# A two-layer encoder on one core: half of the low parts of the up weights subtracted on GpSimd instead of VectorE

## The chip, the cores and the metric

The kernel runs on one core of a Trainium2 chip. A core has TensorE (PE) for matrix products with its own weight loads (PEld), VectorE (DVE), ScalarE (ACT), GpSimd (POOL) and SyncE (SP), which mostly issues DMAs. The metric is the device time of one execution in microseconds (us), of which the median over the runs is taken. Lower is better.

## The reference

The computation is an encoder trunk on 256 tokens of width 2048, with two layers, all in float32:

```python
m = rms_norm(mem, mem_norm)
for i in range(2):
    n = rms_norm(h, attn_norm[i])
    # layer 0: neighbourhood attention, layer 1: grouped-query attention, both beside
    # cross attention from the tokens to 256 memory tokens
    ...
    h = h + concatenate([mix, cross]) @ w_o[i]
    n = rms_norm(h, mlp_norm[i])
    h = h + square(relu(n @ w_up[i])) @ w_down[i]     # 2048 -> 8192 -> 2048
return rms_norm(h, final_norm)
```

The change lies in the MLP, in `n @ w_up[i]`, which runs once in each layer.

## The kernel before

**Precision by splitting.** Products are made in the type fp32r. Each float32 operand is split in two: `hi`, a copy in fp32r made by ScalarE, and `lo`, the difference between the source and `hi`, made by VectorE. A product is then the sum of three: hi*hi, hi*lo and lo*hi. The helper `split` (lines 477 to 480) issues both instructions: line 479 on ScalarE, line 480 on VectorE. So line 480 stands for the low parts of all operands, and the tile names tell them apart.

**The MLP.** The weights of `w_up` come as 64 chunks a layer, each 128x2048 floats in the tile `raw_U` (1 MB, one DMA from SP's queue, line 951). A chunk is used in two halves of 128x1024. `half_of_side` (line 943) takes a pair of tiles `uh` and `ul` for a half, with two buffers for each name, and splits the half of `raw_U` into them. The products of a chunk are 48 matrix products at line 384: for each of 16 blocks, `hi` with two parts of the activations `hT` and `lo` with one, summed in `ps_u`. Behind it ScalarE applies relu and square (lines 1019 and 1020, tile `c`).

Six chunks run ahead (`LEAD = 6`). From then on the kernel works in steps, 58 in each layer. A step has four grains in this order: the first products of a pair chunk of `w_down`, the first and the second half of an up chunk, and the second products of the pair chunk. The pair chunks are computed by Strassen's scheme: four weight blocks `b` (1 MB by DMA) are combined into seven, three of them sums `t` made by VectorE (lines 1072, 1074 and 1075) and one by an accumulating DMA that GpSimd issues (line 1073, `b<-b`). The four blocks in `b` are split into `bh` and `bl`, the three sums into `th` and `tl` (one buffer each). The first grain has 12 products with `bh` and `bl`, the last has 9 with `th` and `tl`. On every second step VectorE also makes four combinations `c` (line 1030) and the split of `a_s`. Steps go in runs (`RUNS`, eight in each layer); at the end of a run the seven PSUM sums are taken over by VectorE (lines 1144 and 1155) and ScalarE (line 1157).

**What sets the order.** Each grain has stages `load`, `pre` and `prep`, which are traced some grains before it runs (`ahead`); the splits of an up half are traced four grains ahead. The order on each engine is then chosen by the scheduler, which simulates the engines' times; `past` and `issue_after` tie some instructions behind others on the same engine. Each engine works its queue in order, and waits in it for what an instruction needs.

Of the kernel before, what the change touches and what calls it, by code (L numbers as in the profile page):

```python
# [10 lines left out]
F32 = mybir.dt.float32  # L11
# [3 lines left out]
ALU = mybir.AluOpType  # L15
# [19 lines left out]
HALF = CH // 2  # L35
# [122 lines left out]
def encoder_kernel(ctx: ExitStack, tc: tile.TileContext, t: dict, out: bass.AP):  # L158
    nc = tc.nc
# [3 lines left out]
    def opened(name, side="left", space=None, bufs=1):  # L163
        kw = {"space": space} if space else {}
        manager = tc.tile_pool(name=name, bufs=bufs, side=side, reuse_waits="tile", **kw)
        pools[name] = manager, manager.__enter__()
        return pools[name][1]

    def closed(*names):
        for name in names:  # L170
            pools.pop(name)[0].__exit__(None, None, None)
# [31 lines left out]
    first = const.tile([P, GAINS + NT * D], F32, name="first")  # L203
# [43 lines left out]
    def halves_of(w):  # L247
# [6 lines left out]
        def prep_early(hf):  # L254
            if w.early == "ring":

                tiles[hf] = new_half(w.kind)
                box["early", hf] = split(*tiles[hf], tiles["raw"][:, hf * HALF : (hf + 1) * HALF])
            else:
                tiles[hf] = half_of_side(tiles["raw"], hf, MOVING_AT)  # L260
# [111 lines left out]
    def products(ps, acts, k0, nk, hi, lo, keep_order=False, first=None):  # L372

        for j in range(nk):
            k = k0 + j
            s = slice(j * P, (j + 1) * P)
            parts = [(hi, slice(0, SEQ)), (hi, slice(SEQ, 512)), (lo, slice(0, SEQ))]
            if k == KT - 1:
                parts[:2] = parts[1::-1]
            elif j == 0 and isinstance(lo, Entered):  # L380
                parts = parts[2:] + parts[:2]
            for n, (x, part) in enumerate(parts):
                x = first if n == j == 0 and first is not None else x[:, s]
                ins = nc.tensor.matmul(ps, x, acts[:, k, part], start=k == n == 0,  # L384
                                       stop=k == KT - 1 and n == 2)
                if keep_order and n == 0:
                    pin(ins)
# [86 lines left out]
            plan.append(Work("M", blocks[b][0][c], acts, c * 4, begins, last, start, blocks[b][1]))  # L474


    def split(dst_hi, dst_lo, src):

        first = nc.scalar.activation(dst_hi, src, AF.Copy)  # L479
        return first, nc.vector.tensor_tensor(dst_lo, src, dst_hi.bitcast(F32), op=ALU.subtract)  # L480

    def rstd_of(ss, n, name):

# [456 lines left out]
    FIRST = ("p3", 6, 0), ("p1", 0, 1), ("p2", 2, 2), ("p5", 3, 3)  # L940
    SECOND = ("p7", 4, 0), ("p6", 5, 1), ("p4", 1, 2)

    def half_of_side(raw, hf, place=0):
        s = slice(place // 4, place // 4 + HALF)
        tiles = tuple(at.side.tile([P, HALF + 64], F32R, tag=n, bufs=2, name=n)[:, s] for n in ("uh", "ul"))
        box.setdefault("splits", []).append(split(*tiles, raw[:, hf * HALF : (hf + 1) * HALF]))
        return tiles

    def loaded(src, tag):
        raw = at.side.tile([P, CH], F32, tag=tag, bufs=2, name=f"raw_{tag}")  # L950
        nc.sync.dma_start(raw, src)
        return raw

    def up_grains(layer, m):
        own = {}
        lead = m < LEAD

        def load():
            own["raw"] = loaded(t[f"w_up{layer}"][m], "U")

        def prep(hf):

            with tc.issue_after(box["summed"].ins) if m in (1, 2) else nullcontext():
                prepared(hf)

        def prepared(hf):
            half = 2 * m + hf
            if lead and (half in (2, 4) or half > 4 and half % 3 == 2):

                if half < 5:  # L970
                    room = at.side.tile([P, 2, HALF], F32R, tag="b", bufs=2, name="u_b")
                    own[hf] = room[:, 0], room[:, 1]
                else:
                    s = slice(U_AT // 4, U_AT // 4 + HALF)
                    own[hf] = tuple(at.mlp.tile([P, 3 * 512], F32R, tag=x, name=f"u_{x}")[:, s] for x in ("th", "tl"))
                box["splits"].append(split(*own[hf], own["raw"][:, hf * HALF : (hf + 1) * HALF]))
            else:
                own[hf] = half_of_side(own["raw"], hf)
            if not lead and hf == 0:

                room = at.side.tile([P, 256], F32R, tag="junk", bufs=1, name="u_0")
                own["first"] = room[:, COPY_AT // 4 :][:, :P]
                nc.scalar.activation(own["first"], own["raw"][:, :P], AF.Copy)

        def run(hf):
            if m == hf == 0:
                closed("cat", "ring")
                at.mlp = opened("mlp")
                box["z"] = [at.mlp.tile([P, 4, 512], F32, tag=f"z{q}", name=f"z{q}") for q in range(2)]
                box["z_set"] = set()  # L990

                last = at.mlp.tile([P, 14 * P], F32R, tag="a", bufs=6, name="hT_l")[:, LAST_COPY_AT // 4 :][:, :SEQ]
                nc.scalar.activation(last, box["hT"][:, KT - 1, :SEQ].bitcast(F32), AF.Copy)
                box["hT0"] = Plain(box["hT"], last)
            if hf == 0:
                if lead:
                    own["ps"] = at.acc.tile([P, 512], F32, tag="acc", name="ps_u")[:, :SEQ]
                else:
                    own["ps"] = sum_of("up")[:, :SEQ]

            with tc.issue_after(box["late"].ins) if m == hf == 0 else nullcontext():
                products(own["ps"], box["hT0" if lead else "hT"], hf * (KT // 2), KT // 2, *own.pop(hf),
                         keep_order=not lead, first=own.pop("first", None))

        def after():
            squared(layer, m, own["ps"])

        soon = (8, 8, 3) if m == 1 else SOONER
        return [Grain(lambda: run(0), None, load, None, lambda: prep(0), soon),
                Grain(lambda: run(1), after, None, None, lambda: prep(1), SOONER)]  # L1010

    def squared(layer, m, ps):

        e = m % 2
        if e == 0:
            box["c"] = at.mlp.tile([P, 8, P], F32, tag="c", bufs=2, name="c")
        c = box["c"]
        two = c[:, 2 * e : 2 * e + 2, :].rearrange("p a b -> p (a b)")
        nc.scalar.activation(two, ps, AF.Relu)
        nc.scalar.activation(two, two, AF.Square)  # L1020
        if e == 0:
            return
        pair = m // 2
        if pair >= max(STEPPED):
            a = at.mlp.tile([P, 2, 4, P], F32R, tag="a", bufs=6, name="a_p")
            split(a[:, 0], a[:, 1], c[:, :4])
        else:
            for d, x, y, op in ((4, 2, 0, ALU.subtract), (5, 1, 0, ALU.add), (6, 5, 2, ALU.subtract),
                                (7, 3, 6, ALU.subtract)):
                box["made"] = nc.vector.tensor_tensor(c[:, d, :], c[:, x, :], c[:, y, :], op=op)  # L1030
            a = at.mlp.tile([P, 2, 7, P], F32R, tag="a", bufs=6, name="a_s")
            split(a[:, 0], a[:, 1], c[:, 1:])
            if pair >= min(STEPPED):

                n = pair - min(STEPPED)
                if n == 0:
                    box["a_0"] = at.mlp.tile([P, max(STEPPED) - min(STEPPED), 2, P], F32R, tag="a", bufs=6, name="a_0")
                split(box["a_0"][:, n, 0], box["a_0"][:, n, 1], c[:, 0])
        box["a", pair] = a
        if m == UPS - 1 and layer == 1:  # L1040
            later(2, load_gf)
# [91 lines left out]
    def sum_of(name):  # L1133
        if name in box["unused"]:
            box["unused"].remove(name)
        else:
            box["ps"][name] = at.sums.tile([P, 512], F32, tag=name, name="ps_u" if name == "up" else name)
        return box["ps"][name]
# [39 lines left out]
    def plain_grains(layer, nb, at_chunk):  # L1178
# [9 lines left out]
        def prep(c, hf):  # L1188
            if (at_chunk + c) % 2 == 0:
                own[c, hf] = half_of_side(own[c], hf, MOVING_AT)  # L1190
            else:
                own[c, hf] = tuple(at.mlp.tile([P, HALF], F32R, tag="bt"[hf] + x, name=f"{x}_p") for x in "hl")
                box["rest"] = split(*own[c, hf], own[c][:, hf * HALF : (hf + 1) * HALF])
# [450 lines left out]
```

## Time and profile before

| | |
|---|---|
| runs | 2001.65 and 2002.13 us, median 2001.89 |
| span of the profiled execution | 1999.8 us, 2.1 us less than the median; the profile gives no other time of this execution |
| TensorE busy in the span | 1989.3 us (99%), 12920 products |
| VectorE busy | 1724.4 us (86%) |
| ScalarE busy | 1276.3 us (64%) |
| GpSimd busy | 123.4 us (6%), of which 100.6 us are 116 DMA issues |
| `ul` subtractions on VectorE | 262, mean 1217 ns, 318.1 us |

Times are those of one profiled execution. A row of a timeline gives the start and the duration of an instruction in us, its engine, the line of the kernel, and the tile it writes `<-` the tiles it reads; behind it, in brackets, how long the engine stood idle before it and what ended the wait. A row of groups gives the number of instructions, their busy time and mean duration, and the idle time before them.

### The profile page before, as it was taken

To read this page: it belongs to the slowest core of one execution; us is meant where nothing else is said; L and a number is where in the kernel's file an instruction comes from. 1 tells how busy PE (TensorE), PEld (TensorE's weight loads), DVE (VectorE), ACT (ScalarE), POOL (GpSimd) and SP (SyncE) were. 2 spreads that over 40 slices of the span, in tenths; PEclk is the share of its full clock that TensorE was granted. 3 is DMA by queue.
4 is the path that set the end of the run, shared out by engine and by line. 5 is a ranking of instruction groups with operands and counts; after the bars stand their busy time and mean duration, and the time that the engine had idled before them with its cause. 6 is when DMAs were issued, how large, how long until landed. Compare 5 with 4: busy or idle time off the path is not lost.

```text
span 1999.8 us, 32844 instructions
## 1 busy us (share of the span) xinstructions
PE 1989.3 (99%) x12920; PEld 1806.9 (90%) x12920; DVE 1724.4 (86%) x2140; ACT 1276.3 (64%) x1735; POOL 123.4 (6%) x145
## 2 busy tenths in 40 slices
PE   9999999999999999999999999999999999999998
PEld 8999999899999999999998888889999999999987
DVE  6777777579998999999999778778998999999997
ACT  6655555467666666666666556666676666666664
POOL 0000000000000000000000001000000000000000
PEclk9999999999999999999999999999999999999999
DMA  7856665757777777777676765557777777777773
GB/s 290 313 192 204 209 208 189 258 175 244 231 228 232 236 234 237 218 238 234 211 232 226 232 234 169 194 177 255 229 227 235 218 235 235 232 239 227 225 227 133
DMA packets 105707, 448.02 MB, mean 224 GB/s; under 512 B 10960, under 2 KB 38608, under 8 KB 58064
## 3 DMA queue, kind: packets, MB, share of 16 engines
q1 hardware_dynamic: 88560, 414.99, 59.4%
q0 software_dynamic: 16704, 30.42, 9.0%
q8 instruction: 101, 1.65, 0.3%
q10 hardware_dynamic: 288, 0.52, 0.1%
q14 instruction: 54, 0.44, 0.1%
HBM read 398.17 MB, written 4.19 MB: 201 GB/s over the span
## 4 chain that ended last, share of the span: by engine, by line
PE 97%; DMA 1%; DVE 1%; issue 1%; ACT 0%; SPq 0%; DVEq 0%; POOLq 0%; POOL 0%; ACTq 0%
PE ps_u L384 34%; PE p L1103 9%; PE p L1104 9%; PE p L1101 9%; PE ps_s L384 9%; PE ps_m L361 8%; PE ps_m L364 8%; PE ps_m L365 8%; DMA raw_l<-in_w_km 0%; PE sc_ps L537 0%; PE sc_ps L538 0%; PE sc_ps L536 0%; PE av L611 0%; PE av L612 0%; PE av L610 0%
## 5 line engine op out<-in xcount | busy, mean ns | idle before, releaser
L384 PE MATMUL ps_u<-hT,uh 128*128 128x256 f32 x3812 | 663.0, 276 | 0.0
L384 PEld LDWEIGHTS ps_u<-hT,uh 128*128 128x128 f32 x3812 | 578.6, 188 | 5.5
L384 PE MATMUL ps_u<-hT,ul 128*128 128x256 f32 x1960 | 541.3, 276 | 0.0
L479 ACT ACTIVATE uh<-raw_U 128x1024 fp32r<-128x1024 f32 x262 | 277.9, 1061 | 238.0 <-PE ps_u L384 226.2
L384 PEld LDWEIGHTS ps_u<-hT,ul 128*128 128x128 f32 x1960 | 368.0, 188 | 0.0
L480 DVE TENSOR_TENSOR lo<-raw,hi 128x1024 fp32r<-128x1024 f32 (+1 forms) x215 | 254.0, 1189 | 96.7 <-ACT hi L479 96.0
L480 DVE TENSOR_TENSOR ul<-raw_U,uh 128x1024 fp32r<-128x1024 f32 x262 | 318.1, 1217 | 19.0 <-ACT uh L479 18.9
L479 ACT ACTIVATE hi<-raw 128x1024 fp32r<-128x1024 f32 (+1 forms) x215 | 221.5, 1036 | 160.6 <-PE ps_m L365 80.8
L479 ACT ACTIVATE bh<-b 128x2048 fp32r<-128x2048 f32 x116 | 222.9, 1922 | 101.5 <-PE p L1104 90.5
L480 DVE TENSOR_TENSOR bl<-b,bh 128x2048 fp32r<-128x2048 f32 x116 | 265.2, 2286 | 12.7 <-ACT bh L479 12.7
L480 DVE TENSOR_TENSOR tl<-t,th 128x1536 fp32r<-128x1536 f32 x116 | 203.4, 1754 | 39.3 <-ACT th L479 38.4
L479 ACT ACTIVATE th<-t 128x1536 fp32r<-128x1536 f32 x116 | 172.9, 1490 | 43.6 <-PE p L1104 41.0
L1103 PE MATMUL p<-bl,a_s 128*128 128x512 f32 x464 | 180.9, 390 | 0.5 <-DVE bl L480 0.3
L1104 PE MATMUL p<-bh,a_s 128*128 128x512 f32 x464 | 181.3, 391 | 0.0
L1101 PE MATMUL p<-bh,a_s 128*128 128x512 f32 x464 | 180.6, 389 | 0.0
L1073 POOL DMA_DIRECT2D b<-b x116 | 100.6, 867 | 1146.9 <-DVE t L1072 939.0
L384 PE MATMUL ps_s<-nT,hi 128*128 128x256 f32 x896 | 154.7, 276 | 0.0
L1101 PE MATMUL p<-th,a_s 128*128 128x512 f32 x348 | 136.1, 391 | 0.0
L1103 PE MATMUL p<-tl,a_s 128*128 128x512 f32 x348 | 135.8, 390 | 0.0
L384 PEld LDWEIGHTS ps_s<-nT,hi 128*128 128x128 f32 x896 | 135.5, 188 | 0.2
L1104 PE MATMUL p<-th,a_s 128*128 128x512 f32 x348 | 135.4, 389 | 0.0
L384 PE MATMUL ps_s<-nT,lo 128*128 128x256 f32 x448 | 123.7, 276 | 0.0
(294 smaller groups left out, 3524.2 us busy)
## 6 DMA issues: line engine op xcount, KB each, us to landing
raw_U<-in_w_up SPq DMA_DIRECT2D x128, 1024.0 KB, 4.9
b<-in_w_pair SPq DMA_DIRECT2D x116, 1024.0 KB, 4.9
raw<-in_w_o SPq DMA_DIRECT2D x32, 1024.0 KB, 5.0
b<-b POOLq DMA_DIRECT2D x116, 256.0 KB, 3.4
raw<-in_w_b SPq DMA_DIRECT2D x21, 1024.0 KB, 5.0
raw<-in_w_av SPq DMA_DIRECT2D x12, 1024.0 KB, 4.9
raw<-in_w_aq SPq DMA_DIRECT2D x12, 1024.0 KB, 5.0
raw<-in_w_ak SPq DMA_DIRECT2D x12, 1024.0 KB, 4.8
```

Of the source, the lines that this page charges most:

```text
L361: first = nc.tensor.matmul(ps, ah, hi[:, s], start=st, stop=False)
L364: nc.tensor.matmul(ps, ah, lo[:, s], start=False, stop=False)
L365: final = nc.tensor.matmul(ps, al, hi[:, s], start=False, stop=sp)
L384: ins = nc.tensor.matmul(ps, x, acts[:, k, part], start=k == n == 0, stop=k == KT - 1 and n == 2)
L479: first = nc.scalar.activation(dst_hi, src, AF.Copy)
L480: return first, nc.vector.tensor_tensor(dst_lo, src, dst_hi.bitcast(F32), op=ALU.subtract)
L1073: nc.gpsimd.dma_start(b[:, 3, :], b[:, 1, :], accum_op=ALU.add)
L1101: ins = nc.tensor.matmul(ps, a[:, 0, ai, :], hi[:, s], start=begins, stop=False)
L1103: nc.tensor.matmul(ps, a[:, 0, ai, :], lo[:, s], start=False, stop=False)
L1104: nc.tensor.matmul(ps, a[:, 1, ai, :], hi[:, s], start=False, stop=ends)
```

## The change

`split` and `half_of_side` take an engine for the subtraction, and `up_grains` passes GpSimd for the second half (`hf` is 1) of the chunks that are not among the first six. 58 chunks in each of two layers are concerned. The copy to `uh` stays on ScalarE, and the buffers, the products and the first half stay as they are.

```diff
-    def split(dst_hi, dst_lo, src):
+    def split(dst_hi, dst_lo, src, engine=None):
 
         first = nc.scalar.activation(dst_hi, src, AF.Copy)
-        return first, nc.vector.tensor_tensor(dst_lo, src, dst_hi.bitcast(F32), op=ALU.subtract)
+        engine = engine or nc.vector
+        return first, engine.tensor_tensor(dst_lo, src, dst_hi.bitcast(F32), op=ALU.subtract)
...
-    def half_of_side(raw, hf, place=0):
+    def half_of_side(raw, hf, place=0, engine=None):
         s = slice(place // 4, place // 4 + HALF)
         tiles = tuple(at.side.tile([P, HALF + 64], F32R, tag=n, bufs=2, name=n)[:, s] for n in ("uh", "ul"))
-        box.setdefault("splits", []).append(split(*tiles, raw[:, hf * HALF : (hf + 1) * HALF]))
+        box.setdefault("splits", []).append(split(*tiles, raw[:, hf * HALF : (hf + 1) * HALF], engine))
         return tiles
...
             else:
-                own[hf] = half_of_side(own["raw"], hf)
+                own[hf] = half_of_side(own["raw"], hf, engine=nc.gpsimd if hf and not lead else None)
```

## The prediction

> **What bounds the kernel now.** I begin with the page's busy times and the chain that ended last, to see whose time the end is.
>
> ```profile
> PE 1989.3 (99%) x12920; PEld 1806.9 (90%) x12920; DVE 1724.4 (86%) x2140; ACT 1276.3 (64%) x1735; POOL 123.4 (6%) x145
> ...
> PE 97%; DMA 1%; DVE 1%; issue 1%; ACT 0%; SPq 0%; DVEq 0%; POOLq 0%; POOL 0%; ACTq 0%
> ```
>
> TensorE is the bound: 1989.3 of 1999.8 us, and 97% of the chain. VectorE carries 1% of it, so taking work off VectorE can win at most a little: 1999.8 - 1989.3 = 10.5 us of idle PE is all there is, 0.5%. The open question is what the change costs. For that the stage counts where the changed line runs, so the second view is the table by stretches: two long stretches of the MLP (one per layer), and one pair of steps.
>
> ```profile
> core 0: us, PE busy (x) PEld busy (x) DVE busy (x) ACT busy (x) POOL busy (x), PEclk, DMA share, GB/s
> 500.00:1000.00 500.00, 500.00 (x3377) 459.04 (x3375) 465.43 (x502) 336.43 (x374) 42.60 (x49) 1.00 0.73 230
> 1400.00:1900.00 500.00, 500.00 (x3374) 459.01 (x3373) 465.39 (x504) 336.41 (x374) 42.15 (x49) 1.00 0.74 230
> 541.25:561.71 20.46, 20.46 (x140) 18.79 (x139) 18.29 (x20) 13.69 (x16) 1.74 (x2) 1.00 0.72 229
> ```
>
> PE never rests here and its clock is full. VectorE is busy 465.4 of 500 us, so it is the second bound: a step of one up chunk and one pair chunk takes 20.46 / 2 = 10.23 us, in which VectorE works 10.23 x 465.4 / 500 = 9.52 us and rests 0.71 us. From the order of VectorE's work in that pair of steps:
>
> ```profile
> 547.34 1.21 DVE L480 TENSOR_TENSOR ul<-raw_U,uh 128x1024 fp32r<-128x1024 f32 x1
> 548.48 0.68 DVE L1075 TENSOR_TENSOR t<-t,b 128x512 f32<-128x512 f32 x1
> 549.08 1.22 DVE L480 TENSOR_TENSOR ul<-raw_U,uh 128x1024 fp32r<-128x1024 f32 x1
> 550.21 0.28 DVE L1030 TENSOR_TENSOR c<-c 128x128 f32<-128x128 f32 x1
> 551.48 1.76 DVE L480 TENSOR_TENSOR tl<-t,th 128x1536 fp32r<-128x1536 f32 x1 [0.99 <-ACT th L479]
> ...
> 554.65 2.29 DVE L480 TENSOR_TENSOR bl<-b,bh 128x2048 fp32r<-128x2048 f32 x1
> ...
> 559.12 1.23 DVE L480 TENSOR_TENSOR ul<-raw_U,uh 128x1024 fp32r<-128x1024 f32 x1 [0.44 <-ACT uh L479]
> 560.26 0.81 DVE L1030 TENSOR_TENSOR c<-c 128x128 f32<-128x128 f32 x3
> ```
>
> The second `ul` of each step (549.08 and 559.12) is the one that the change moves. Each frees 550.21 - 549.08 = 1.13 us of VectorE's line (an instruction starts 0.08 us before the one ahead of it ends). Almost everything else in the line is a tensor_tensor with both inputs in SBUF.
>
> **The change part by part.** *Removed from VectorE:* 58 chunks behind the first six in each of two layers, 116 subtractions by 1.13 us, 131 us in all, or 1.13 us a step. None of it lies on PE's chain, so alone it is worth nothing.
>
> *Added on GpSimd:* 116 subtractions of 128x1024. No row shows such an instruction there. What GpSimd does show:
>
> ```profile
> L227 POOL MEMSET ones<- 128x128 f32 x1 | 0.2, 204 | 0.3 <-POOLq L1634 0.3
> L229 POOL MEMSET mhalf<- 128x8 f32 x1 | 0.1, 104 | 0.0
> ```
> ```profile
> L1407 POOL TENSOR_SCALAR b_r_r<-b_r_r,rstd x8: 302/436/1369, 1135.5 to 1228.3; 128x4 f32<-128x4 f32 x8
> ```
>
> From the two memsets one stream costs (204 - 104) / 120 = 0.83 ns an element, 0.85 us for 1024, and the shortest small two-operand instruction gives 0.30 us to start and end. If the two inputs and the output all run beside one another, that is 1.15 us; if the inputs follow each other, 2.0 us; if all three do, 2.85 us. Ends 1.15 and 2.85; the rows do not say whether the store hides, and I take the middle of the upper two, 2.4 us. [...]
>
> *Does it run beside VectorE?* If it did, GpSimd's 6% load would take it in easily. These rows speak against it:
>
> ```profile
> 405.40 0.69 POOL L852 TENSOR_TENSOR scale<-near,mhalf 128x2 f32<-128x2 f32 x1 [333.09 <-DVE near L836]
> ...
> 1094.66 3.88 POOL L1298 TENSOR_TENSOR rstd<-full,mhalf 128x2 f32<-128x2 f32 x1 [65.57 <-DVE full L836]
> ```
> ```profile
> 1094.47 1.23 DVE L480 TENSOR_TENSOR lo<-raw,hi 128x1024 fp32r<-128x1024 f32 x1
> 1095.61 1.23 DVE L480 TENSOR_TENSOR ul<-raw_U,uh 128x1024 fp32r<-128x1024 f32 x1
> 1096.74 1.23 DVE L480 TENSOR_TENSOR lo<-raw,hi 128x1024 fp32r<-128x1024 f32 x1
> 1098.58 0.17 DVE L1454 TENSOR_SCALAR qm_s<-rstd 128x2 f32<-128x2 f32 x1 [0.60 <-POOL rstd L1298]
> ```
>
> The same power of two numbers takes 0.69 us with VectorE idle and 3.88 us when three subtractions run on VectorE without a gap. It ends at 1098.54, 0.57 us after the last of them (1097.97). So GpSimd waits for a gap in VectorE's two-input work, and most of its 0.69 us still lies ahead of it then; some 0.12 us of its start is hidden by the wait. Whether VectorE in turn waits while GpSimd reads is what the sum hangs on. One row leans against it:
>
> ```profile
> 1227.12 1.04 POOL L488 TENSOR_TENSOR b_r_r<-b_r_v,mhalf 128x4 f32<-128x4 f32 x1 [0.92 <-DVE b_r_v L486]
> ```
> ```profile
> 1227.83 0.69 DVE L1412 TENSOR_TENSOR b_o<-b_y,cos_q 128x512 f32<-128x512 f32 x1 [0.79 <-ACT b_y L1410]
> ```
>
> Here a VectorE product starts inside a GpSimd instruction and is not stretched; but that one reads four numbers a partition, which it may have done long before 1227.83. The bounds for VectorE's wait are 0 and the whole hold. I take the whole hold, as an engine that is kept off something by its neighbour most likely keeps the neighbour off as well.
>
> [...]
>
> *The sum.* Per step VectorE loses 2.4 - 0.12 = 2.28 us to the hold and 0.08 us of overlap at the break, and is spared 1.13: a net 1.23 us. It has 0.71 us of rest, so 0.52 us a step do not fit: 116 x 0.52 = 60 us. Against that stands the lead with which VectorE now works. `bl` ends at 554.65 + 2.29 = 556.94; the product that reads it:
>
> ```profile
> L1103 PE MATMUL p<-bl,a_s 128*128 128x512 f32 x464 | 180.9, 390 | 0.5 <-DVE bl L480 0.3
> ```
> ```profile
> 549.99 0.39 PE L1103 MATMUL p<-bl,a_s 128*128 128x512 f32 x1
> ```
>
> The first read of the next `bl` comes a period later, at 560.2, 3.3 us after its making; two layers give 2 x 3.3 = 7 us of lag for free. VectorE's work from PSUM at the ends of runs may partly go on during a hold:
>
> ```profile
> L1144 DVE SCALAR_TENSOR_TENSOR first<-p,inv,first 128x512 f32<-128x512 f32 x48 | 35.8, 746 | 3.1 <-PE p L1104 1.1
> L1155 DVE TENSOR_TENSOR z<-p,z 128x512 f32<-128x512 f32 x48 | 32.8, 684 | 1.1 <-PE p L1104 1.1
> ```
>
> That is 68.6 us in 16 bursts of 4.3 us; each burst could hide 1 us of a hold, but also spends more than the 3.3 us lead at once, and I set the two against each other. The sum: 60 - 7 = +53 us. The profiled span is 1999.8 us, so 2053; the median of the runs is 2.1 us longer than this span, so the time shown should be **2055 us**, +2.6%.
>
> *Queues and covers.* The subtraction waits on GpSimd for `uh` (ACT), and behind it stands the accumulating DMA of the next pair chunk (L1073), for which ACT's `bh` waits.
>
> ```profile
> 554.50 0.87 POOL L1073 DMA_DIRECT2D b<-b  x1 [8.48 <-DVE t L1072]
> ```
> ```profile
> b<-b POOLq DMA_DIRECT2D x116, 256.0 KB, 3.4
> ```
> ```profile
> 558.02 1.06 ACT L479 ACTIVATE uh<-raw_U 128x1024 fp32r<-128x1024 f32 x1 [1.66 <-PE ps_u L384]
> ...
> 562.91 1.92 ACT L479 ACTIVATE bh<-b 128x2048 fp32r<-128x2048 f32 x1 [0.40 <-PE p L1104]
> ```
>
> GpSimd rested 8.48 us ahead of that issue; a subtraction from 559.1 to 561.5 is over before the next issue near 565, and the landed data (554.50 + 3.4 = 557.9) waits 5 us for `bh`. I cost the queue at nothing; with the subtraction more than 5 us late the DMA, `bh`, `bl` and PE are late in turn. The subtraction's own latency is covered too:
>
> ```profile
> 552.65 5.45 PE ps_u L384 x48
> ```
>
> The up products of a chunk take 5.45 us, so the second half starts at 552.65 + 2.72 = 555.4, and a step later at 565.6, 4 us behind the subtraction's end at 561.5. SP's queue and ACT's work are unchanged.
>
> **The rivals.** *(A) Forecast:* both exclude each other and the sum overflows VectorE's rest. With the subtraction between 2.1 and 2.65 us the time is 2020 to 2085; at its upper end of 2.85 us the same sum gives 2107.
>
> *(B) Not slower: VectorE isn't held up.* GpSimd only waits for a gap and then reads beside VectorE. For it: the unstretched row at 1227.83, and the two gaps that a step already has (0.99 and 0.44 us in the lines above, and 1.13 us more where `ul` was). Then VectorE gets 1.13 us of rest, PE stays the bound: 2002 us, between 1995 and 2008. It decides from the point at which VectorE's instructions keep their 1.22 us beside a GpSimd subtraction.
>
> *(C) The hold is short.* Mutual exclusion, but inputs and output overlap: at 1.15 to 2.0 us VectorE's net is 0.0 to +0.8 us a step against 0.71 of rest, so 0 to 10 us: 2002 to 2012.
>
> *(D) GpSimd is starved.* Once VectorE lags, its line has no gap, and the subtraction that misses the gap ahead of `tl` waits until the one behind the next `ul`, at 558.7 in the lines above; it would end at 561.1, while PE wants it at 555.4: 6 us of PE idle. One step in six so would cost 19 x 6 = 114 us: 2116. For it speaks the 3.88 us row; against it, that a stalled PE gives VectorE gaps again.
>
> That the change does not do what it says (the subtractions stay, or the order written by the scheduler moves other work) I hold for small; the time would be 2002 or anything near.
>
> **How the numbers follow.** A 0.54, of which 0.42 lies above +2% (2042 us) and 0.12 below; B 0.20; C 0.10; D 0.14; the rest 0.02, split evenly. Slower by over 2%: 0.42 + 0.14 + 0.01 = 0.57. Within 2%, which is about what a measurement of this kernel can tell from no change: 0.12 + 0.20 + 0.10 = 0.42. Faster by over 2% has no room in 10.5 us of idle PE: 0.01. The range runs from B (1998) to somewhat beyond D's middle (2125), leaving out B's lowest and a starvation worse than one step in six. The likeliest case's own range is 2020 to 2085.
>
> **What the changed profile would show.** Under A: POOL rows `ul<-raw_U,uh` x116 of 2.3 to 2.6 us, VectorE rows beside them stretched or preceded by idle time that POOL ends, VectorE plus POOL near 100% in the MLP stretches, and PE idle ahead of L1103 `p<-bl` or L384 `ps_u<-hT,ul`. Under B: VectorE's durations unchanged, its busy time 131 us less, PE at 99%. Under C: POOL rows below 2 us. Under D: POOL rows of 4 us and more, and PE's idle time ahead of `ps_u<-hT,ul` alone, ended by POOL. I am wrong above all if the GpSimd subtraction is far slower than three streams (a conversion to fp32r in its loop), or if VectorE is free during it.

## The result and the profile after

The changed kernel takes 2032.94 us (median of 2032.09 and 2033.79) against 2001.89 us: a ratio of 1.0156, 95% interval 1.0126 to 1.0185. It is slower by 31 us, 1.6%: inside the stated range, on the forecast side of no change, but not past 2%, which the prediction held the likelier outcome (0.57); the forecast was 2055 us. The profiled execution took 2033.79 us with a span of 2032.0 us.

The page's lines on busy times, on the chain that ended last, and on the costliest groups that moved:

```profile
PE 1999.7 (98%) x12920; PEld 1813.0 (89%) x12920; DVE 1793.5 (88%) x2024; ACT 1270.8 (63%) x1735; POOL 541.2 (27%) x261
...
PE 77%; DVE 12%; issue 4%; DMA 3%; POOL 3%; ACT 1%; DVEq 0%; SPq 0%; POOLq 0%; ACTq 0%
...
L384 PE MATMUL ps_u<-hT,ul 128*128 128x256 f32 x1960 | 545.7, 278 | 20.6 <-POOL ul L481 17.8
...
L481 POOL TENSOR_TENSOR ul<-raw_U,uh 128x1024 fp32r<-128x1024 f32 x116 | 417.3, 3597 | 261.1 <-ACT uh L479 261.1
...
L481 DVE TENSOR_TENSOR tl<-t,th 128x1536 fp32r<-128x1536 f32 x116 | 238.2, 2054 | 18.0 <-ACT th L479 17.8
...
L1031 DVE TENSOR_TENSOR c<-c 128x128 f32<-128x128 f32 x240 | 144.6, 622 | 5.2 <-ACT c L1021 3.4
```

(The lines behind 480 are one higher than before.) VectorE has 116 instructions less and 69 us more busy time: its `c` rows went from 284 to 622 ns, its `tl` rows from 1754 to 2054. So VectorE is held while GpSimd subtracts. And PE now stands 17.8 us ahead of products with `ul`, released by GpSimd, where it stood not at all.

How the hold looks in a regular pair of steps, GpSimd's timeline and then VectorE's:

```profile
550.20 3.55 POOL L481 TENSOR_TENSOR ul<-raw_U,uh 128x1024 fp32r<-128x1024 f32 x1 [2.28 <-ACT uh L479]
...
560.43 2.60 POOL L481 TENSOR_TENSOR ul<-raw_U,uh 128x1024 fp32r<-128x1024 f32 x1 [3.15 <-ACT uh L479]
```
```profile
550.60 0.68 DVE L1076 TENSOR_TENSOR t<-t,b 128x512 f32<-128x512 f32 x1
551.20 0.29 DVE L1031 TENSOR_TENSOR c<-c 128x128 f32<-128x128 f32 x1
552.68 2.68 DVE L481 TENSOR_TENSOR tl<-t,th 128x1536 fp32r<-128x1536 f32 x1 [1.20 <-ACT th L479]
...
559.54 1.22 DVE L481 TENSOR_TENSOR ul<-raw_U,uh 128x1024 fp32r<-128x1024 f32 x1
561.09 2.61 DVE L1031 TENSOR_TENSOR c<-c 128x128 f32<-128x128 f32 x3 [0.33 <-ACT c L1021]
```

At 550.20 GpSimd's instruction begins, but VectorE's `t` and `c` keep their durations: GpSimd gets in only when VectorE's line breaks at 551.5. It then runs to 553.75, and `tl`, which starts at 552.68, ends 0.92 us late (2.68 against 1.76). At 560.43 VectorE's `ul` is nearly done: it ends at 560.76, a break follows, GpSimd gets in and runs to 563.03, and the three `c` take 2.61 us instead of 0.81. The pair costs VectorE 0.92 + 1.80 = 2.72 us, and spares it two subtractions of 1.13. The rest of the hold lies in VectorE's own waits for ScalarE (1.20 and 0.33 us). PE loses nothing here: the step is 10.23 us as before.

Where the 31 us are lost shows in the length of the steps, from the start of one chunk's up products to the next. Of 57 steps in the first layer these are the ones in which the kernels of this study stand out most, and ahead of them 5 and 13, the second steps behind the first two run ends. Steps are counted from 0; runs end in the steps 3, 11, 19, 27, 35, 43, 51 and 57. The last two lines are all that lies over 10.23 us a step in each layer. The other columns are the experiments below, in the order of their runs but for the one with both halves on GpSimd; each column is one profiled execution.

```
step  before  after  skip5   half   copy memset    mid   ends  first   rest no_ends
   5   10.23  10.23  10.23  10.22  10.23  10.23  10.23  10.23  10.22  10.22  10.22
  13   10.22  10.23  10.23  10.23  10.23  10.23  10.22  10.23  10.23  10.23  10.23
  21   10.23  11.44  10.23  10.23  10.22  10.23  10.22  10.72  17.23  10.23  10.23
  23   10.23  10.23  10.76  10.22  10.23  10.23  11.26  10.23  10.22  10.44   10.22
  24   10.23  10.89  10.22  10.23  10.22  10.23  10.22  10.22  10.23  11.40  10.23
  29   10.23  12.04  10.23  10.22  10.23  10.23  10.23  10.61  17.10  10.23  10.22
  37   10.22  12.30  10.23  10.23  10.23  10.22  10.22  10.63  17.12  10.23  10.23
  40   10.22  11.44  10.22  10.22  10.23  10.23  10.23  10.22  10.23  10.23  10.23
  45   10.23  12.23  10.24  10.23  10.22  10.23  10.23  11.01  17.23  10.22  10.23
  52   10.62  11.16  11.28  10.25  10.23  10.22  10.64  11.72  13.02  10.63  10.23
  53   10.23  15.40  17.56  18.89  11.30  10.23  10.22  15.45  15.93  10.23  10.22
sum1     0.4   16.9   12.3    8.7    1.1    0.0    3.7    8.8   42.0    1.8    0.6
sum2     1.0   16.4   12.1    8.4    2.5    0.0    4.5    9.2   46.2    1.4    0.0
```

The changed kernel loses 33.3 - 1.4 = 31.9 us in the steps, nearly all of the 32.2 us between the two spans, and 24 of it in the second steps behind the ends of runs: 1.2 to 2.1 us in 21, 29, 37 and 45, and 5.2 us in 53. Most other steps are as long as before. Steps 5 and 13 lose nothing: behind the run ends 3 and 11 VectorE takes over only three sums (line 1145), behind the later ones seven (lines 1145 and 1156). One of the places where PE waits, VectorE, GpSimd and PE:

```profile
755.46 2.29 DVE L481 TENSOR_TENSOR bl<-b,bh 128x2048 fp32r<-128x2048 f32 x1
757.66 0.69 DVE L1075 TENSOR_TENSOR t<-t,b 128x512 f32<-128x512 f32 x1
758.27 1.09 DVE L481 TENSOR_TENSOR a_s<-c,a_s 128x896 fp32r<-128x896 f32 x1
759.27 1.22 DVE L481 TENSOR_TENSOR ul<-raw_U,uh 128x1024 fp32r<-128x1024 f32 x1
760.40 0.69 DVE L1076 TENSOR_TENSOR t<-t,b 128x512 f32<-128x512 f32 x1
761.01 0.29 DVE L1031 TENSOR_TENSOR c<-c 128x128 f32<-128x128 f32 x1
761.21 1.76 DVE L481 TENSOR_TENSOR tl<-t,th 128x1536 fp32r<-128x1536 f32 x1
763.00 2.74 DVE L1073 TENSOR_TENSOR t<-b 128x512 f32<-128x512 f32 x1
```
```profile
757.98 7.21 POOL L481 TENSOR_TENSOR ul<-raw_U,uh 128x1024 fp32r<-128x1024 f32 x1 [1.26 <-ACT uh L479]
```
```profile
765.24 0.39 PE L384 MATMUL ps_u<-hT,ul 128*128 128x256 f32 x1 [1.53 <-POOL ul L481]
```

VectorE is behind from the sums of the run that ended, and its line has no break from 757.66 to 762.97; then comes one of 0.03 us. GpSimd's subtraction, ready at 757.98, gets in only there, 5.0 us later, takes 2.2 us (VectorE's next `t` takes 2.74 us instead of 0.69), and ends at 765.19; PE stood idle for it from 763.71.

How far VectorE is ahead shows why here. Its lead is the time from the end of a `bl` to the start of the first product that reads it. Worked out from these rows for the pair chunks of the steps around the run end in step 27 (`ends` and `no_ends` are experiments below):

```
step       26    27    28    29    30    31    32    33    34    35    36    37
before   3.28  3.17  2.48  2.90  2.29  2.64  2.87  3.17  3.27  3.17  2.48  2.90
after    1.55  1.63  1.36  0.35  1.47  1.17  1.18  1.47  1.62  1.68  1.41  0.15
ends     3.28  3.17  2.48  2.41  1.46  1.18  1.70  2.85  3.28  2.95  2.48  2.41
no_ends  2.53  2.60  2.74  2.66  2.81  2.65  2.80  2.66  2.81  2.65  2.80  2.66
```

In the kernel before, a run's end takes 0.9 us of the lead, and by step 33 it is back. In the changed kernel VectorE comes to the run's end with half of it, has 0.35 us left in step 29, regains 1.1 us only as PE stands still there, and from step 30 to 35 gains 0.2 us where it gained 0.9 before.

A thin lead makes other delays count as well. Ahead of the steps 24 and 40, which lose 0.7 and 1.2 us, VectorE had waited 0.94 and 1.58 us for the DMA of `b`. The row ahead of step 40, and a like one of the kernel before, where step 38 and those behind it lose nothing:

```profile
871.16 0.69 DVE L1073 TENSOR_TENSOR t<-b 128x512 f32<-128x512 f32 x1 [1.58 <-DMA b<-in_w_pair]
```
```profile
851.65 0.69 DVE L1072 TENSOR_TENSOR t<-b 128x512 f32<-128x512 f32 x1 [1.48 <-DMA b<-in_w_pair]
```

### The profile page after: what moved, and what is told of

The parts are those of the page before. It is cut to its first block, busy times and chain, and to the rows that moved or that the text cites. A ratio compares the mean times of both kernels' runs of the same rounds, so it can differ in the third digit from the quotient of the medians.

```text
span 2032.0 us, 32807 instructions
## 1 busy us (share of the span) xinstructions
PE 1999.7 (98%) x12920; PEld 1813.0 (89%) x12920; DVE 1793.5 (88%) x2024; ACT 1270.8 (63%) x1735; POOL 541.2 (27%) x261
## 4 chain that ended last, share of the span: by engine, by line
PE 77%; DVE 12%; issue 4%; DMA 3%; POOL 3%; ACT 1%; DVEq 0%; SPq 0%; POOLq 0%; ACTq 0%
PE ps_u L384 24%; PE ps_s L384 10%; PE ps_m L361 8%; PE ps_m L365 8%; PE ps_m L364 8%; PE p L1105 6%; PE p L1102 6%; PE p L1104 6%; POOL ul L481 3%; DVE ul L481 2%; DMA b<-in_w_pair 2%; DVE tl L481 2%; DVE t L1076 2%; DVE c L1031 1%; DVE t L1073 1%
## 5 line engine op out<-in xcount | busy, mean ns | idle before, releaser
L384 PE MATMUL ps_u<-hT,ul 128*128 128x256 f32 x1960 | 545.7, 278 | 20.6 <-POOL ul L481 17.8
L481 POOL TENSOR_TENSOR ul<-raw_U,uh 128x1024 fp32r<-128x1024 f32 x116 | 417.3, 3597 | 261.1 <-ACT uh L479 261.1
L481 DVE TENSOR_TENSOR tl<-t,th 128x1536 fp32r<-128x1536 f32 x116 | 238.2, 2054 | 18.0 <-ACT th L479 17.8
L481 DVE TENSOR_TENSOR ul<-raw_U,uh 128x1024 fp32r<-128x1024 f32 x146 | 215.4, 1476 | 6.6 <-ACT uh L479 6.6
L1031 DVE TENSOR_TENSOR c<-c 128x128 f32<-128x128 f32 x240 | 144.6, 622 | 5.2 <-ACT c L1021 3.4
L1102 PE MATMUL p<-th,a_s 128*128 128x512 f32 x348 | 136.1, 391 | 0.0
```

The source lines that it names most:

```text
L481: return first, engine.tensor_tensor(dst_lo, src, dst_hi.bitcast(F32), op=ALU.subtract)
L1102: ins = nc.tensor.matmul(ps, a[:, 0, ai, :], hi[:, s], start=begins, stop=False)
```

## The experiments

The theory after these traces (S): GpSimd and VectorE exclude each other, a regular step hides it, and the loss comes from subtractions that get no turn behind the end of a run, where VectorE's line has no break. The rival (T) is the prediction's sum: the two engines have more work in every step than fits. A third (O) puts the waits down to the scheduler, which orders VectorE's queue otherwise where it knows of the change. PE's and SP's orders are the same before and after; VectorE's, the missing `ul` aside, is the same in regular steps and differs behind the run ends, where some 15 instructions (`bl`, `t`, `a_s`, `c`, `tl`) are put in another order, and in the steps 51 to 57; ScalarE's differs there too. Where no interval is given, the time of an experiment is that of one execution.

**Five chunks back on VectorE.**

```diff
-                own[hf] = half_of_side(own["raw"], hf, engine=nc.gpsimd if hf and not lead else None)
+                away = m - LEAD in (21, 29, 37, 45, 53)
+                own[hf] = half_of_side(own["raw"], hf, engine=nc.gpsimd if hf and not lead and not away else None)
```

> As the changed kernel, but in each layer the second halves of the five chunks 21, 29, 37, 45 and 53 behind the lead go back to VectorE (106 of 116 subtractions stay on GpSimd). Theory S (starvation): GpSimd gets in only where VectorE's two-input work has a gap, VectorE has none behind a run's end, and the time is lost in the one subtraction there that PE then waits for. In the changed trace these ten steps take 24 us more than 10.23 us each, all others 8 us together, so S expects 2033 - 24 = 2009 us (2003 to 2014). Theory T (throughput, the sum of the prediction): VectorE and GpSimd together have more work in every step than fits, so a tenth less on GpSimd gives a tenth of the loss back and the wait moves to a step beside: 2030 us (2025 to 2033).

Measured: 2023.52 us, ratio 1.011 (1.0093 to 1.0127). Neither. The steps 21, 29, 37 and 45 are at 10.23 us, as S says, with 0.3 to 0.8 us lost in some steps beside them. But step 53 went from 15.4 to 17.6 us, and another wait stands there, in PE's timeline:

```profile
1019.68 0.80 PE L1105 MATMUL p<-bl,a_s 128*128 128x512 f32 x1 [4.82 <-DVE bl L481]
```

PE now waits for VectorE's `bl`. VectorE was late with `bl` because it did the returned `ul` and was then held by the next chunk's subtraction on GpSimd. So it isn't only GpSimd that comes late: at the end of the last run but one, where the most work from the sums meets, VectorE's lead is 0.05 us in step 53 of the kernel before too, and more work for it is paid by PE.

**Half the width.**

```diff
-        engine = engine or nc.vector
-        return first, engine.tensor_tensor(dst_lo, src, dst_hi.bitcast(F32), op=ALU.subtract)
+        if engine is None:
+            return first, nc.vector.tensor_tensor(dst_lo, src, dst_hi.bitcast(F32), op=ALU.subtract)
+        a, b = slice(0, HALF // 2), slice(HALF // 2, HALF)
+        engine.tensor_tensor(dst_lo[:, a], src[:, a], dst_hi[:, a].bitcast(F32), op=ALU.subtract)
+        return first, nc.vector.tensor_tensor(dst_lo[:, b], src[:, b], dst_hi[:, b].bitcast(F32), op=ALU.subtract)
```

> As the changed kernel, but GpSimd subtracts only the first 512 of the 1024 columns of the second half and VectorE the other 512. The hold falls from 2.3 to about 1.2 us. Theory S: the wait for a gap in VectorE's line stays (some 5 us at the run ends), only the hold behind it is shorter: ten stalls lose about 1.1 us each: 2033 - 11 = 2022 us (2012 to 2026). Theory T: per step VectorE loses 1.2 + 0.08 and is spared 0.57, a net of 0.7 against 0.71 of rest, which fits: 2002 us (2001 to 2006).

Measured: 2016.37 us. The number is in S's range, but not for its reason: ten steps of 1.1 us less were expected, and instead eight stalls vanished and the ninth and tenth grew to about 8.5 us each. GpSimd's rows with this tile, and PE's:

```profile
L483 POOL TENSOR_TENSOR ul<-raw_U,uh x116: 1298/1917/13002, 455.4 to 1962.7; 128x512 fp32r<-128x512 f32 x116
```
```profile
1011.47 0.58 PE L384 MATMUL ps_u<-hT,ul 128*128 128x256 f32 x1 [6.70 <-POOL ul L483]
```

One subtraction of 1.3 us lasted 13.0 us, since it got no turn for 12 us, in which VectorE's line had no break. This is rival D of the prediction at its purest.

**Writing only, and one input only.**

```diff
-        engine = engine or nc.vector
-        return first, engine.tensor_tensor(dst_lo, src, dst_hi.bitcast(F32), op=ALU.subtract)
+        if engine is None:
+            return first, nc.vector.tensor_tensor(dst_lo, src, dst_hi.bitcast(F32), op=ALU.subtract)
+        for a in range(0, HALF, HALF // 2):
+            last = engine.memset(dst_lo[:, a : a + HALF // 2].bitcast(F32), 0.0)
+        return first, last
```

> The subtraction on GpSimd is replaced by two memsets of 512 columns each of the same tile: GpSimd only writes, and the low part of these halves is left out of the computation. If it is reading that excludes the engines, nothing waits for anything: VectorE's rows keep their durations, the memsets theirs (about 0.5 us each), and the time is 2002 us (2000 to 2004). If any work of GpSimd excludes VectorE's two-input work, the memsets wait for a gap as the subtraction did and the run ends stall by some 0.5 us: 2010 to 2020 us.

Measured: 1999.47 us, 2.2 us below its kernel before. The memsets take 522 to 851 ns, median 530, and VectorE's `tl` keeps 1756 ns. PE waits for none of it; so it is reading that excludes the engines in this kernel. The time is also about the most that taking the subtraction off VectorE could have brought. And it takes O out as a cause by itself: VectorE's order in this kernel, and in the next one, is that of the changed kernel, row for row behind the run ends too, and with that order every step from 21 to 53 is at 10.23 us here. Whether the order of before would make the exclusion cheaper behind the ends was not tried.

```diff
-        engine = engine or nc.vector
-        return first, engine.tensor_tensor(dst_lo, src, dst_hi.bitcast(F32), op=ALU.subtract)
+        if engine is None:
+            return first, nc.vector.tensor_tensor(dst_lo, src, dst_hi.bitcast(F32), op=ALU.subtract)
+        return first, engine.tensor_copy(dst_lo, dst_hi)
```

> The subtraction on GpSimd is replaced by a copy of the high part into the same tile: one stream read, one written, and the low part of these halves is not computed. If reading excludes the engines, the copy waits for a gap as the subtraction does, takes 1.0 to 1.4 us from then on, VectorE's rows are stretched beside it, and the run ends still stall, by less than with two inputs: 2015 us (2006 to 2025). If it takes two inputs on GpSimd to collide, VectorE's rows keep their durations and the time is 2002 us (2000 to 2004).

Measured: 2003.21 us, in the range of the other theory, that it takes two inputs to collide. The durations say otherwise:

```profile
L482 POOL CAST ul<-uh x116: 1042/1084/7352, 457.5 to 1949.5; 128x1024 fp32r<-128x1024 f32 x116
```
```profile
L1032 DVE TENSOR_TENSOR c<-c x240: 273/291/1126, 436.3 to 1922.6; 128x128 f32<-128x128 f32 x120
```

One input on GpSimd was enough to exclude here: a copy of 1.04 us lasted up to 7.35, and a `c` of 0.29 us up to 1.13. But the copy is so short that regular steps keep most of their rest, and little is left over behind the run ends: 3.6 us over all steps.

**Only the middle of the runs, and only behind the ends.**

```diff
-                own[hf] = half_of_side(own["raw"], hf, engine=nc.gpsimd if hf and not lead else None)
+                n = m - LEAD
+                away = n % 8 in (4, 5, 6) or n >= 50
+                own[hf] = half_of_side(own["raw"], hf, engine=nc.gpsimd if hf and not lead and not away else None)
```

> GpSimd subtracts only in the middle of the runs: the chunks n behind the lead with n mod 8 equal to 4, 5 or 6 and all from 50 on (26 of 58 in a layer) go back to VectorE, 64 of 116 subtractions stay on GpSimd. Theory L (local): a subtraction on GpSimd costs VectorE a net 1.2 us, hidden wherever VectorE has rest, and it reaches PE only behind the ends of runs, where VectorE has none. L expects 2002 us (2001 to 2006) and no step of PE over 10.6 us that the kernel before does not have. Theory T (the loss is spread over all subtractions): 2002 + 31 x 64 / 116 = 2019 us. Theory O (order: the scheduler's other order of VectorE's queue makes the waits, as VectorE's late bl in step 53 of the kernel with five chunks moved back suggests): waits come up at other steps, 2008 to 2025 us.

Measured: 2011.22 us, ratio 1.0051 (1.0034 to 1.0067). It lies between L and T, and inside O's range, and the memsets do not answer O here, as VectorE's order in this kernel is not theirs. The steps behind the run ends lose nothing more; instead the steps 23, 31, 39 and 47 lose up to 1.2 us, where PE waits for VectorE's own `ul`. These come four steps behind a run's end: VectorE's lead is 1.01 us in step 22 and 0.37 in step 23, behind the end in step 19, so the backlog still stands there and the subtractions from n mod 8 = 7 on add to it.

The reverse puts `and ends` in the place of `and not away`, with the same condition.

> The reverse: GpSimd subtracts only in the 26 chunks of a layer behind the ends of runs (n mod 8 equal to 4, 5 or 6, and all from 50 on), 52 of 116; the others stay on VectorE. Theory L: nearly the whole loss remains, 2028 us (2020 to 2036), and it stands in the steps 20 to 24, 28 to 32, 36 to 40, 44 to 48 and 52 to 54. Theory T: 2002 + 31 x 52 / 116 = 2016 us.

Measured: 2018.03 us, below L and near T by the number. The place is L's: 18.0 us are over the steps, nearly all in 21, 29, 37, 45 (0.4 to 0.8 us), 52 and 53. But the stalls in 21 to 45 are a quarter of those of the changed kernel, though the same subtractions stand on GpSimd there. The steps ahead of a run's end matter as well: in the table of leads VectorE comes to step 27 with 3.17 us here and with 1.63 us in the changed kernel, where the rest of the steps ahead is spent on holds. The two losses, 8.2 and 18.0, add up to 26 of 33; the 8.2 is of the fastest of four executions, 3 us below their median.

**Both halves.**

```diff
-                own[hf] = half_of_side(own["raw"], hf, engine=nc.gpsimd if hf and not lead else None)
+                own[hf] = half_of_side(own["raw"], hf, engine=nc.gpsimd if not lead else None)
```

> Both halves of the chunks behind the lead are subtracted on GpSimd, 232 subtractions. Theory L: in a regular step VectorE rests 1.08 us, is spared 2 x 1.13 us and is held 2 x 2.35 us: 1.4 us a step do not fit, now in every step: 116 x 1.4 = 160 us, 2160 us (2110 to 2200). If the engines exclude each other only at GpSimd's cost (it waits, VectorE does not): 2002 to 2040 us. If only the run ends matter, twice the loss of the changed kernel: 2065 us.

Measured: 2238.16 us, more than L's range. Now regular steps do not fit: about every fourth step (14 of 57 in the first layer) takes 16.5 to 18.5 us, with PE waiting for `bl`.

```profile
483.07 0.80 PE L1104 MATMUL p<-bl,a_s 128*128 128x512 f32 x1 [4.58 <-DVE bl L481]
...
532.33 0.79 PE L1104 MATMUL p<-bl,a_s 128*128 128x512 f32 x1 [5.33 <-DVE bl L481]
```
```profile
core 0: us, PE busy (x) PEld busy (x) DVE busy (x) ACT busy (x) POOL busy (x), PEclk, DMA share, GB/s
483.00:487.00 4.00, 3.93 (x9) 3.14 (x10) 3.97 (x7) 0.95 (x1) 0.00 (x0) 0.50 0.76 252
```

PE's waits for VectorE sum to 145.2 us for `bl` and 12.9 for `tl`, just about the 160 that were expected. What had been left out is the clock: behind the wait of 4.58 us PE ran at half speed (0.50 from 483 to 487). All steps together lose 238 us, so some 80 us stand beside the waits. The mean granted clock of the run, 0.960 instead of 0.999, gives 87 us over 2236.4 us, a part of which passes during the waits.

**The first half in place of the second.**

```diff
+                own[hf] = half_of_side(own["raw"], hf, engine=nc.gpsimd if not hf and not lead else None)
```

> The first half of the chunks goes to GpSimd and the second stays on VectorE: the same number of subtractions at another place of the step, where VectorE's line is about to run bl, t and ul. Theory L: the same hold against the same rest: 2033 us (2022 to 2045). If the place decides (GpSimd's request comes when VectorE's line has no gap until the next ul is done), PE waits for ul in many regular steps too: 2050 to 2150 us.

Measured: 2087.86 us. The number is in the range of the theory of place, but its words are not right: regular steps do not wait. The second steps behind the run ends do, at 17.1 to 17.4 us from 21 to 45, with a wait of 4.3 us and a slow clock behind it (0.50 from 684 to 688):

```profile
684.72 0.58 PE L384 MATMUL ps_u<-hT,ul 128*128 128x256 f32 x1 [4.40 <-POOL ul L481]
```

PE reads the first half 2.7 us before the second, so the same lateness of GpSimd costs more: 4.29 us against 1.53 in step 29. The steps 3 and 11, where a run ends, lose 1.7 to 2.5 us too, with PE waiting for `bl`.

**Only the rested steps, and no run ends.** The refined theory (L): the subtractions take the rest of regular steps, and PE pays what is left of a burst.

```diff
+                n = m - LEAD
+                rested = n % 8 < 4 and 8 <= n < 50
+                own[hf] = half_of_side(own["raw"], hf, engine=nc.gpsimd if hf and rested else None)
```

> GpSimd subtracts only where VectorE has had time to rest since the last run end: the chunks n behind the lead with n mod 8 below 4 and n from 8 to 49, 22 of 58 in a layer, 44 of 116. The refined theory L (a subtraction on GpSimd takes VectorE's rest of a regular step, and PE waits only where a backlog from a run end is still there, as at the steps 23, 31 and 39 of the kernel with 64 on GpSimd) expects no wait of PE that the kernel before does not have: 2002 us (2001 to 2004). A loss in proportion to the number, from the kernel with 64: 2001 + 10 x 44 / 64 = 2008 us.

Measured: 2004.53 us (2003.36 to 2007.09 over ten runs), ratio 1.0017 (1.0007 to 1.0027). Below proportion (2008), above L's range (2001 to 2004), so L's "no wait of PE" is missed: in the profiled execution, the fastest of the ten, step 24 loses 1.2 us. There VectorE had stood idle 1.81 us ahead of 699.32 for the DMA of `b`, with the lead down to 0.05 us. VectorE's order, `ul` aside, is that of the kernel with 64, row for row, so 20 subtractions less, and not another order, bring the loss in the steps from 8.2 to 3.2 us. The ten runs scatter over 3.7 us where the runs of before scatter over 2.1. That the DMA makes this scatter too is likely but was not tried.

```diff
-            if ends and j == STEPPED[q] - 1:
+            if False:
                 folded(q, 0.5 if n == len(STEPS) - 1 else 2)
...
         if name in DIRECT:
             i, b = DIRECT[name]
-            add_scaled(columns_of(i, q, b), ps, inv[:, i : i + 1])
             return
...
-            nc.vector.tensor_tensor(z, ps, z, op=ALU.add)
+            return
```

> The changed kernel with all 116 subtractions on GpSimd, but VectorE's work at the ends of runs is left out: the PSUM sums of the pair products are not added to the residual and to z, nor is z folded in, so this part of the MLP is missing from the output. Theory L: without the bursts VectorE's rest of 1.08 us a step takes every hold, PE waits nowhere: 2001 us (1999 to 2005), and GpSimd's subtractions last under 5 us everywhere. If regular steps do not fit either (the prediction's 0.52 us a step): 2030 us and more.

> The same work left out of the kernel before, for comparison: PE has no wait for VectorE in the steps even with that work, but for 0.4 us at step 52 of each layer, so 2000 us (1998 to 2002). The difference between this run and the changed kernel without the run ends is what the subtractions on GpSimd cost in regular steps.

Measured: 2001.14 us with all 116 subtractions on GpSimd, and 2000.34 us for the kernel before without the same work. The same window of the first and of the second, with columns as above, and the subtractions of the first:

```profile
500.00:1000.00 500.00, 500.00 (x3377) 459.20 (x3377) 476.53 (x418) 336.75 (x373) 177.22 (x99) 1.00 0.74 232
```
```profile
500.00:1000.00 500.00, 500.00 (x3378) 459.20 (x3377) 448.17 (x466) 337.09 (x375) 42.73 (x49) 1.00 0.74 232
```
```profile
L481 POOL TENSOR_TENSOR ul<-raw_U,uh x116: 2390/2861/3843, 458.4 to 1947.4; 128x1024 fp32r<-128x1024 f32 x116
```

PE has no rest, no subtraction lasts over 3.84 us, and VectorE is busy or held for 476.5 of 500 us, against 448.2 without the change. So the change costs VectorE 28.4 us there, 0.58 us a step, out of a rest of 1.06. That settles T: a regular step takes the hold without loss (0.8 us between the two kernels, over 116 steps). The loss of the changed kernel needs the bursts at the run ends. VectorE's order is the same in the two kernels, so with the bursts the scheduler's other order is gone too; whether that order adds to what the exclusion costs behind the run ends stays open.

## Why the prediction was right, and where it was not

**The bound and the gain.** Right. PE was the bound, and without any exclusion the kernel gains 2.2 us (the memsets), within the 10.5 us that were allowed.

**The price of a subtraction.** Right: 2.4 us were taken between 1.15 and 2.85, and the shortest row is 2.394 us; that it fits so closely is luck, as the rows behind it left the whole range open. At half width it is 1.298, so 2.14 ns an element and 0.20 us to start and end.

**Mutual exclusion.** Right, and this carried the forecast; the whole hold was the author's choice between two bounds. The row at 1227.83 that spoke against it fits with the way out that the prediction gave, that GpSimd had read its four numbers by then; no run shows this itself. The runs show the exclusion on both sides: VectorE's rows are stretched (three `c` from 0.81 to 2.61 us), GpSimd's last up to 9.54 us where the shortest takes 2.39, and the memsets, which only write, are not concerned (median 530 ns, with VectorE's `tl` at 1756 ns beside them). Which of the two starts first does not settle whose turn it is: the subtraction of 757.98 was passed over by VectorE instructions that started later, up to the one that ends at 762.97. Nor does the prediction's "GpSimd waits for a gap" hold throughout, as the last section shows.

**The sum.** This is the step that failed: "a net 1.23 us. It has 0.71 us of rest, so 0.52 us a step do not fit: 116 x 0.52 = 60 us". The 0.71 us is a mean over 500 us in which the run ends lie. The regular pair in the same fence rests 20.46 - 18.29 = 2.17 us, so 1.08 a step, and with that only 0.15 us a step do not fit. The net of 1.23 us is too large as well: the runs without the ends measure 0.58 us a step, since a part of the hold falls into VectorE's own waits for ScalarE, as in the pair above, and the sum did not take that off. So 0.58 stand against 1.06, and every regular step fits. The term that the prediction dropped, the 16 bursts "set against each other", is where the loss begins: what a burst takes of the lead of 3.3 us was formerly won back in the rest of the next steps, and this rest is now spent on holds, so that the next burst meets half a lead (1.63 us ahead of step 27). So two errors of opposite sign: 60 us where there is nothing in regular steps, and nothing where there are 32 us. That the forecast missed by 22 us only is in part luck.

**The rivals.** A and D each have half of it: A's exclusion is the cause, and D's starvation the form in which most of the loss reaches PE. Of D's 19 waits of 6 us there are ten of 0.8 to 3.3 us released by GpSimd, 17.8 us of idle PE in all. D's own argument against itself, "a stalled PE gives VectorE gaps again", holds: the step behind each stall is at 10.23. B and C are out. The scheduler did move other work, which the prediction held for small: by the memsets that order alone costs nothing.

**The signs.** "POOL rows of 2.3 to 2.6 us" were right for the short ones (2.39), but the median is 3.28, the wait for a turn being part of the row. "Idle time ahead of `ps_u<-hT,ul`, ended by POOL" was given for D and is what came.

**What was not seen.** Two waits, of 3.27 and 3.28 us, also cost the clock. Behind the 3.27 us wait in step 53:

```profile
1020.95 0.38 PE L384 MATMUL ps_u<-hT,ul 128*128 128x256 f32 x1 [3.27 <-POOL ul L481]
```
```profile
1021.00:1023.00 2.00, 2.00 (x12) 2.00 (x13) 2.00 (x2) 0.00 (x0) 0.88 (x1) 0.70 0.53 98
1023.00:1025.00 2.00, 2.00 (x11) 2.00 (x11) 2.00 (x3) 0.00 (x0) 0.00 (x0) 0.50 1.03 383
1025.00:1027.00 2.00, 2.00 (x10) 1.68 (x10) 1.71 (x3) 1.75 (x3) 0.62 (x1) 0.95 1.07 260
```

In windows of 2 us from 1021 on the granted clock (the third number from the end of each line) is 0.70, 0.50 and 0.95: 1.7 us lost, and as much behind the 3.28 us wait of the second layer (0.60 and 0.55 from 1943 on).

## What to carry to other kernels

Taking work from a busy VectorE to an idle GpSimd freed nothing here, where VectorE's instructions have two inputs in SBUF and GpSimd's read SBUF: without the run ends VectorE was busy or held for 476.5 of 500 us with the change and for 448.2 without. Where a trace shows the like, count the two as one engine for such instructions, at GpSimd's longer duration (2.39 us against 1.22 for this subtraction). And measure the rest that is to hide a cost in the regular steps and in the bursts apart: a mean over both hides the place where the cost is paid. GpSimd's instruction was also passed over for long while VectorE's line had no break (5.0 us, 12 us at half the width), so it belongs where VectorE waits for something, not behind a burst, and not on what TensorE reads next.

## What the runs showed of the hardware

GpSimd was not served in turn beside VectorE's two-input instructions. Where these followed without a break it was passed over by several: for 5.0 us from 757.98 on, and for 12 us in the run with half the width. But a break wasn't always needed. In 54 of the 116 rows GpSimd gets in between two such instructions, the second of which begins before the first has ended (mostly by 0.08 us, as in the kernel before), and is then stretched:

```profile
746.63 2.50 POOL L481 TENSOR_TENSOR ul<-raw_U,uh 128x1024 fp32r<-128x1024 f32 x1 [1.40 <-ACT uh L479]
```
```profile
746.18 0.68 DVE L1075 TENSOR_TENSOR t<-t,b 128x512 f32<-128x512 f32 x1
746.78 3.43 DVE L481 TENSOR_TENSOR ul<-raw_U,uh 128x1024 fp32r<-128x1024 f32 x1
```

What decides between the two cases was not found. In the ten rows for which PE waited, GpSimd got in only at a break, of 0.03 us in nine of them and 0.21 in one.

VectorE's instructions with one input from PSUM were not held. GpSimd's and VectorE's timelines of the changed kernel at a run's end:

```profile
736.40 4.18 POOL L481 TENSOR_TENSOR ul<-raw_U,uh 128x1024 fp32r<-128x1024 f32 x1 [1.67 <-ACT uh L479]
```
```profile
738.01 0.29 DVE L1031 TENSOR_TENSOR c<-c 128x128 f32<-128x128 f32 x1
738.22 0.74 DVE L1145 SCALAR_TENSOR_TENSOR first<-p,inv,first 128x512 f32<-128x512 f32 x1
738.88 0.68 DVE L1156 TENSOR_TENSOR z<-p,z 128x512 f32<-128x512 f32 x1
739.47 2.72 DVE L481 TENSOR_TENSOR tl<-t,th 128x1536 fp32r<-128x1536 f32 x1
```

GpSimd ends at 740.58, so with its 2.2 to 2.4 us it got in at about 738.3, when `c` was done. Within that hold the two instructions that read `p` from PSUM keep their 0.74 and 0.68 us, and only `tl`, with both inputs in SBUF, is held up, by 0.96 us. In this trace 31 instructions of these two lines lie at least in part in the last 2.3 us of a row of GpSimd's; they take 0.74 to 0.75 us (line 1145) and 0.68 to 0.69 us (line 1156), as in the kernel before (0.746 and 0.684 in the mean).

PE's clock halved (0.50) behind waits of 3.27 us (changed kernel), 4.40 us (first half on GpSimd) and 4.58 us (both halves); behind the wait of 1.53 us in the changed kernel it is 1.00. The length of the wait alone does not decide: in the run with the first half on GpSimd it is 1.00 behind one of 2.50 us, and 0.50 from 2025 to 2027, behind one of 2.00 us that ended at 2023.24. Behind the 3.27 us wait it is slow for about 3.4 us (1.7 us lost at half speed), behind the 4.40 us wait for 4.9 us: 0.50, 0.50 and 0.59 in windows of 2 us from 684 on. What sets it was not found.
